# Order of the memory's products in a hybrid layer: values first, and the keys' norm and transposes inside the first attention step

## The chip, the cores and the metric

One NeuronCore of a Trainium2 chip runs the whole program; the seven others are idle. The metric is the time of one execution on the device in microseconds (us). The kernel before takes 1273.12 us, the median of three runs.

## The reference

One layer of a streaming encoder on x (512 rows of 1024 features) with a memory of 256 rows. In float32:

```python
x = x + 0.5 * swiglu(rmsnorm(x, ffn1_norm), ...)          # feed-forward 1
h = rmsnorm(x, mix_norm)
aq, ak, av, bq, bk, bv, cq = split(h @ w_in)
o_a = diff_attention(rope(norm(aq)), rope(norm(ak)), av, lam)  # A, block-causal
o_b = chunk_band_attention(norm(bq), norm(bk), bv, b_rel_bias) # B, band of chunks
mk, mv = split(rmsnorm(mem, mem_norm) @ w_mem_kv, 2)      # memory: keys, values
o_c = memory_attention(norm(cq), norm(mk), mv)            # C: 4 heads of 128
gates = sigmoid(h @ w_gate + b_gate)
x = x + (sum of gates * (branches @ w_branch)) @ w_out
x = x + 0.5 * swiglu(rmsnorm(x, ffn2_norm), ...)          # feed-forward 2
return rmsnorm(x, final_norm)
```

`norm` is an RMS norm of each head with a gain. `lam` is one number, made from two dot products of learned vectors.

## The kernel before

**Products.** Every float32 operand of a product is held as two parts, a high part (`whi`, `mwh`, `fh`, `hh`, ...) that ACT casts (L77) and a low part that DVE gets by subtracting (L78). A product is three matmuls (`mm3`, L110 to L112): high by high, and the two mixed ones. Weights come by DMA from SyncE's queue into a ring of six raw buffers (`wraw`), are split, and used.

**Stages.** Feed-forward 1 is first. In its last part each row block t of x (128 rows, four of them) is finished by DVE (L271, `x_sb`), and `row_mix` at once makes that block's norm for the attentions: square on ACT (L137), `ms` on DVE (L156), the power -1/2 on POOL (`rs`, L121), the scaled row `xn` on DVE (L141, two halves), two groups of four transposes on PE into banks "t" (L149), and the split of these into `hh` (ACT) and `hl` (DVE). The memory's rows were normed earlier and lie transposed in `mh`, `ml`.

Then come three products with a helper, `rows_product`, which takes weights in four chunks: the memory's keys (`mk_ps`, two row tiles in the two banks "s", 48 matmuls of 512 columns), the attention queries against the memory (`cq_ps`, four row tiles in banks "p", "g", "g", "o", 96 matmuls), and the memory's values (`mv_ps`, again the two banks "s", 48 matmuls). Keys and cq are normed by head (`norm4`): a square on ACT (L576), a sum on DVE (L578, `hss`), `msh` on DVE (L127), a power on POOL (L121, `rsh`), the scaling on DVE, which reads the bank (L580), and the gain on DVE (L586). `heads_T` (L593) transposes a normed tile on PE and splits it, for the keys into `mkh`, `mkl`. L618 to L624 make `lam`. ACT copies the values out of their banks (L629).

**The order of the work.** On PE the attentions stand in an order written out by hand: strings like PLAN_C0 name what PE does in one step of a unit. `p4` is four steps of the unit's projection (three matmuls of 384 columns each), `f2` two steps of the gates and branches (three matmuls of 512 columns each), and `c.qt`, `c.sc`, `c.sc2`, `c.pt`, `c.pv` are the stages of one row block of the memory attention: transposes of cq, scores of two heads, scores of the other two, transposes of the probabilities, product with the values. PLAN_C0 is the string of the first unit's step, step 0. Everything else, the rows above among it, is ordered by the Tile scheduler, engine by engine; inside `tc.high_priority(offset=AHEAD)` an instruction is ranked 600 places earlier. Each engine runs its list in that order, and what an instruction must wait for is set by the tiles that it reads, and by the banks and buffers that it takes over (banks: "s" 2, "g" 2, "p" 1, "o" 1, "t" 2).

Of the kernel before, what the change touches and what calls it, by code (L numbers as in the profile page):

```python
# [11 lines left out]
F32 = mybir.dt.float32  # L12
# [6 lines left out]
P = 128  # L19
# [7 lines left out]
NMT = NM // P  # L27
EPS = 1e-6
NEG = -1e30
AHEAD = 600  # L30


PLAN_C0 = "p2 c.qt p2 c.sc p2 f4 c.sc2 p3 f2 c.qt f2 c.pt f4 c.pv"
PLAN_C = "c.sc f1 p2 u.ot c.ot p2 u.pt c.sc2 p2 u.qt p3 c.qt f1 u.sc f1 c.pt f1 u.pv f1 c.pv"
PLAN_A = "c.sc p2 c.ot c.sc2 p3 u.pt p2 u.qt u.ot p2 c.pt f2 u.sc f1 u.pv c.pv f3"
PLAN_B = "p5 u.pt p2 u.qt u.ot p2 f1 u.sc f1 u.pv f4"
# [11 lines left out]
def layer_kernel(ctx: ExitStack, tc: tile.TileContext, a: dict, out: bass.AP):  # L48
    nc = tc.nc

    base = ctx.enter_context(tc.tile_pool(name="base", bufs=1))
# [8 lines left out]
    def bank(tag):  # L60
        return pp.tile([P, 512], F32, tag=tag, name="ps_" + tag, bufs=BANKS[tag])
# [13 lines left out]
    def split(raw, hi, lo, engine=None):  # L75

        nc.scalar.copy(out=hi, in_=raw)  # L77
        (engine or nc.vector).tensor_tensor(out=lo, in0=raw, in1=f32(hi), op=ALU.subtract)  # L78
# [22 lines left out]
    def weight(src, n, pool=None, tags=("whi", "wlo"), bufs=4, raw=None, engine=None):  # L101
        if raw is None:
            raw = load(src, n)
        hi, lo = ((pool or base).tile([P, 1024], F32R, tag=t, name=t, bufs=bufs)[:, :n] for t in tags)
        split(raw, hi, lo, engine)
        return hi, lo

    def mm3(ps, st, mv, first, last):

        nc.tensor.matmul(ps, lhsT=st[0], rhs=mv[0], start=first, stop=False)  # L110
        nc.tensor.matmul(ps, lhsT=st[0], rhs=mv[1], start=False, stop=False)  # L111
        return nc.tensor.matmul(ps, lhsT=st[1], rhs=mv[0], start=False, stop=last)  # L112
# [201 lines left out]
    class Job:  # L314


        def __init__(self, prep, run, blocks=1):
            self.prep, self.run, self.blocks = prep, run, blocks
# [233 lines left out]
    h2, mT = mix_in["h"], mix_in["mT"]  # L552
# [3 lines left out]
    mem_pool = memp.__enter__()  # L556

    def heads(ap, n):
        return ap.rearrange("p (h d) -> p h d", h=n)


    def rows_product(acc, actT, w, c0, **where):

        for c in range(4):
            wc = weight(w[c * 256:(c + 1) * 256, c0:c0 + 512].rearrange("(k p) n -> p k n", p=P), 1024, **where)
            for t, ps in enumerate(acc):
                for j in range(2):
                    k, o = 2 * c + j, slice(j * 512, j * 512 + 512)
                    mm3(ps, tuple(m[:, k, t * P:(t + 1) * P] for m in actT), (wc[0][:, o], wc[1][:, o]),
                        k == 0, k == ND - 1)  # L570
        return acc

    def head_norm(src, dst, sq):

        nh, hd = src.shape[1], src.shape[2]
        nc.scalar.activation(out=sq, in_=src, func=AF.Square)  # L576
        ss = tiny("hss", nh)
        nc.vector.tensor_reduce(out=ss, in_=sq, axis=AX.X, op=ALU.add)  # L578
        rs = rsqrt_mean(ss, nh, 1.0 / hd, "h")
        nc.vector.tensor_tensor(out=dst, in0=src, in1=rs.unsqueeze(2).broadcast_to([P, nh, hd]), op=ALU.mult)  # L580

    def norm4(ps, yn, sq, gain):

        head_norm(heads(ps, 4), heads(yn, 4), heads(sq, 4))
        v = heads(yn, 4)
        nc.vector.tensor_tensor(out=v, in0=v, in1=gain.unsqueeze(1).broadcast_to([P, 4, 128]), op=ALU.mult)  # L586
        return yn

    def heads_T(yn, dst, cols):

        ps = bank("t")
        for h in range(4):
            nc.tensor.transpose(ps[:, h * P:(h + 1) * P], yn[:, h * P:(h + 1) * P], ident)  # L593
        split(heads(ps, 4), dst[0][:, :, cols], dst[1][:, :, cols])

    mem_w = dict(pool=mem_pool, tags=("mwh", "mwl"), bufs=2)
    gck, gcq = (mem_pool.tile([P, P], F32, name="gc" + n) for n in "kq")
    for g, n in ((gck, "k"), (gcq, "q")):
        nc.sync.dma_start(out=g, in_=a[f"c_{n}_norm"].partition_broadcast(P))
    mkT = [base.tile([P, 4, NM], F32R, tag="w4", name=n, bufs=2) for n in ("mkh", "mkl")]  # L600
    mk_ps = rows_product([bank("s") for _ in range(NMT)], mT, a["w_mem_kv"], 0, **mem_w)
    for t in range(NMT):
        yn = mem_pool.tile([P, 512], F32, tag="mk", name="mk", bufs=3)
        sq = mem_pool.tile([P, 512], F32, tag="mk", name="mksq", bufs=3)
        heads_T(norm4(mk_ps[t], yn, sq, gck), mkT, slice(t * P, (t + 1) * P))
    cq_ps = rows_product([bank(t) for t in ("p", "g", "g", "o")], h2, a["w_in"], 3072)
    y_sb = base.tile([P, ND, S], F32, tag="xy", name="y_sb")

# [1 line left out]
    for t in range(NT):  # L610
        sq = mem_pool.tile([P, 512], F32, tag="mk", name="cqsq", bufs=3)
# [11 lines left out]

    nc.vector.tensor_scalar(out=nlam, in0=le[:, 1:2], scalar1=-LAMBDA_INIT, scalar2=le[:, 0:1],  # L624
                            op0=ALU.add, op1=ALU.subtract)
    mv_ps = rows_product([bank("s") for _ in range(NMT)], mT, a["w_mem_kv"], 512, **mem_w)
    mv = base.tile([P, NMT, 512], F32, tag="kx", name="mv", bufs=2)
    for t in range(NMT):
        nc.scalar.copy(out=mv[:, t, :], in_=mv_ps[t])  # L629
    memp.__exit__(None, None, None)  # L630
    mix_in["mTp"].__exit__(None, None, None)
    norm_pool[0] = (base, "raw", 6)
# [9 lines left out]
    def bcast(name, src, n):  # L642
        g = mp.tile([P, n], F32, name=name)
        nc.sync.dma_start(out=g, in_=src.partition_broadcast(P))
        return g

    gsub = bcast("gsub", a["a_sub_norm"], 128)
    nc.vector.tensor_scalar(out=gsub, in0=gsub, scalar1=1.0 - LAMBDA_INIT, scalar2=None, op0=ALU.mult)
    gb = mp.tile([P, 2, 64], F32, name="gb")
# [23 lines left out]

    def p_tile(name):
        return mp.tile([P, 512], F32, tag="p", name=name, bufs=4)

    def pT_tile(name):
        return mp.tile([P, 512], F32, tag="pT", name=name, bufs=2)
# [10 lines left out]
    def new_oT(name):  # L689

        return (mo.tile([P, 4, S], F32R, tag="oh", name=name + "h", bufs=2),
                mo.tile([P, 4, S], F32R, tag="ol", name=name + "l", bufs=2))
# [12 lines left out]
    class MemStep:  # L705
# [16 lines left out]
        def scores(self, hp):  # L722
            s_ps = bank("g")
            sv = heads(s_ps, 2)
            for j in range(2):
                h = 2 * hp + j
                mm3(sv[:, j, :], tuple(v[:, h, :] for v in self.cq), (mkT[0][:, h, :], mkT[1][:, h, :]), True, True)
            nm = tiny("nm", 2)
            nc.vector.tensor_reduce(out=nm, in_=sv, axis=AX.X, op=ALU.max, negate=True)
            nc.vector.tensor_scalar(out=nm, in0=nm, scalar1=C_SCALE, scalar2=None, op0=ALU.mult)  # L730
            pt = p_tile("p")
            for j in range(2):
                h = 2 * hp + j
                nc.scalar.activation(out=heads(pt, 2)[:, j, :], in_=sv[:, j, :], func=AF.Exp, scale=C_SCALE,
                                     bias=nm[:, j:j + 1], accum_out=self.sum[:, h:h + 1])
            self.pts.append(pt)
# [214 lines left out]
    def advance(gen, n):  # L951
        for _ in range(n):
            next(gen, None)
# [8 lines left out]
    def due(kind, stage):  # L962

        most = 1 if stage == "qt" and kind == "c" else NT
        steps = todo[kind, stage][:most]
        del todo[kind, stage][:most]
        for st in steps:
            with tc.high_priority(offset=AHEAD):
                getattr(st, stage)()
            if stage in nxt[kind]:  # L970
                todo[kind, nxt[kind][stage]].append(st)

    def born(kind, step):
        todo[kind, "qt"].append(step)

    def run(step, plan):

        work = {"p": step.proj() if step else fill, "f": fill}
        for item in plan.split():
            if "." in item:  # L980
                due(*item.split("."))
            else:
                advance(work[item[0]], int(item[1:]))
        if step:
            born("u", step)
# [19 lines left out]
    with tc.manual_schedule(engines={mybir.EngineType.PE}):  # L1005
# [3 lines left out]
        for u in range(8):  # L1009
            un = Unit(u)  # L1010
            for i in range(NT):
                if u in (0, 4) and i == 2:
                    oTs.append(new_oT("o" + "ab"[u // 4]))
                run(UnitStep(un, i), (PLAN_C0 if i == 0 else PLAN_C) if u == 0 else PLAN_A if u < 4 else PLAN_B)
        for _ in range(3):
# [112 lines left out]
```

## Time and profile before

| what | value |
|---|---|
| median of 3 runs | 1273.12 us (1272.8 to 1274.1) |
| the profiled execution | 1273.05 us |
| its span | 1271.3 us |
| mean granted clock of TensorE | 0.987 |
| PE busy | 1232.4 us, 97% |
| DVE, ACT, POOL busy | 842.8, 596.8, 107.1 us |
| chain that ended last | PE 90%, DVE 4%, DMA 2% |

The span runs from the first to the last instruction on the core; 1.75 us of the execution lie outside it. A timeline has one line per instruction, or per run of like ones: start, duration, engine, line, operation, tile written and tiles read, and in brackets the idle time of the engine before it and what released it. Durations of one engine overlap a little at the ends, so what one of several costs is the distance from start to start. The granted clock is a share of full speed: 1.00 is 2.4 GHz, 0.50 is 1.2 GHz.

### The profile page before, as it was taken

What the parts mean: (1) busy time and instruction counts of PE and PEld (TensorE: products, weight loads), DVE (VectorE), ACT (ScalarE), POOL (GpSimd) and SP (SyncE); (2) the same over time, 40 slices, a digit from 0 to 9 for tenths busy, and PEclk for the clock granted to TensorE, in tenths of its full rate; (3) what the DMA queues carried; (4) which work ended last, traced back from release to release, by engine and by line L of the source; (5) the groups of instructions that cost most, each with busy time, mean ns of one, the idle gap of its engine ahead of it and who ended that gap; (6) DMA issues with size and microseconds to landing.
All of it is one profiled execution on the core that took longest, in us unless ns stands there. A gap on an engine that the chain in (4) does not pass through costs nothing.

```text
span 1271.3 us, 19657 instructions
## 1 busy us (share of the span) xinstructions
PE 1232.4 (97%) x7808; PEld 1116.9 (88%) x7808; DVE 842.8 (66%) x1377; ACT 596.8 (47%) x1115; POOL 107.1 (8%) x108
## 2 busy tenths in 40 slices
PE   7799999999998999999999999999979999999997
PEld 7789989989986799999999999888878998998996
DVE  7977667667564756766765565453697766766753
ACT  7535425435443446554555454443463452543543
POOL 1100000000000301111221121020000000000002
PEclk8899999999999899999999999999989999999999
DMA  5533324322334403321222320254133242342311
GB/s 215 174 108 116 115 71 128 113 91 101 116 118 130 109 28 108 88 67 58 88 87 70 89 83 31 75 159 160 34 127 122 76 133 91 101 129 73 130 35 67
DMA packets 53084, 127.57 MB, mean 100 GB/s; under 512 B 10112, under 2 KB 10624, under 8 KB 52992
## 3 DMA queue, kind: packets, MB, share of 16 engines
q1 hardware_dynamic: 52416, 125.27, 30.9%
q8 instruction: 61, 1.00, 0.3%
q10 hardware_dynamic: 576, 1.05, 0.2%
q14 instruction: 31, 0.25, 0.1%
HBM read 122.11 MB, written 4.19 MB: 99 GB/s over the span
## 4 chain that ended last, share of the span: by engine, by line
PE 90%; DVE 4%; DMA 2%; ACT 1%; POOL 1%; issue 1%; SPq 0%; POOLq 0%; ACTq 0%; DVEq 0%
PE ps_s L354 19%; PE ps_g L110 9%; PE ps_g L112 9%; PE ps_g L111 9%; PE ps_o L354 5%; PE ps_p L110 4%; PE ps_p L354 4%; PE ps_p L111 4%; PE ps_p L112 4%; PE ps_g L354 4%; PE ps_s L110 2%; PE ps_s L112 2%; PE ps_s L111 2%; PE ps_o L881 2%; PE ps_s L849 2%; PE ps_t L697 1%
## 5 line engine op out<-in xcount | busy, mean ns | idle before, releaser
L77 ACT CAST whi<-wraw 128x1024 fp32r<-128x1024 f32 (+1 forms) x120 | 119.0, 993 | 141.3 <-PE ps_s L354 68.6
L78 DVE TENSOR_TENSOR wlo<-wraw,whi 128x1024 fp32r<-128x1024 f32 (+1 forms) x120 | 137.9, 1151 | 65.6 <-ACT whi L77 64.6
L354 PE MATMUL ps_s<-mhi,whi 128*128 128x256 f32 x496 | 138.3, 279 | 2.3 <-ACT snap L397 2.0
L354 PE MATMUL ps_s<-mlo,whi 128*128 128x256 f32 x496 | 137.7, 278 | 0.0
L354 PE MATMUL ps_s<-mhi,wlo 128*128 128x256 f32 x496 | 136.8, 278 | 0.0
L77 ACT CAST whi<-quarter 128x1024 fp32r<-128x1024 f32 x54 | 56.7, 1051 | 91.8 <-PE ps_s L354 22.7
L354 PEld LDWEIGHTS ps_s<-mhi,whi 128*128 128x128 f32 x496 | 93.8, 189 | 4.1 <-ACT snap L397 2.8
L110 PE MATMUL ps_p<-whi,hh 128*128 128x384 f32 (+1 forms) x264 | 94.8, 359 | 0.0
L354 PEld LDWEIGHTS ps_s<-mlo,whi 128*128 128x128 f32 x496 | 93.7, 189 | 1.0 <-DVE mlo L78 0.2
L354 PEld LDWEIGHTS ps_s<-mhi,wlo 128*128 128x128 f32 x496 | 93.2, 189 | 0.0
L112 PE MATMUL ps_p<-whi,hl 128*128 128x384 f32 (+1 forms) x264 | 89.2, 338 | 0.0
L111 PE MATMUL ps_p<-wlo,hh 128*128 128x384 f32 (+1 forms) x264 | 89.2, 338 | 0.0
L78 DVE TENSOR_TENSOR wlo<-quarter,whi 128x1024 fp32r<-128x1024 f32 x54 | 65.9, 1221 | 24.5 <-ACT whi L77 24.5
L110 PE MATMUL ps_g<-hh,fh 128*128 128x512 f32 x192 | 78.4, 408 | 0.0
L112 PE MATMUL ps_g<-hh,fl 128*128 128x512 f32 x192 | 75.8, 395 | 0.0
L111 PE MATMUL ps_g<-hl,fh 128*128 128x512 f32 x192 | 75.7, 394 | 0.0
L834 DVE CAST kx<-ps_t 128x256 fp32r<-128x256 f32 x32 | 13.6, 425 | 83.7 <-PE ps_t L832 83.7
L121 POOL TENSOR_TENSOR rsh<-msh,mhalf 128x4 f32<-128x4 f32 x38 | 45.2, 1191 | 276.9 <-DVE msh L127 225.2
L78 DVE TENSOR_TENSOR fl<-wraw,fh 128x768 fp32r<-128x768 f32 x48 | 50.0, 1042 | 26.1 <-ACT fh L77 26.1
L77 ACT CAST fhi<-quarter 128x1024 fp32r<-128x1024 f32 x34 | 35.5, 1049 | 59.1 <-PE ps_s L354 16.4
L354 PE MATMUL ps_s<-mhi,fhi 128*128 128x256 f32 x208 | 59.2, 285 | 2.5 <-ACT fhi L77 2.5
L354 PE MATMUL ps_s<-mlo,fhi 128*128 128x256 f32 x208 | 58.9, 283 | 0.0
(376 smaller groups left out, 3662.8 us busy)
## 6 DMA issues: line engine op xcount, KB each, us to landing
wraw<-in_ffn_w SPq DMA_DIRECT2D x88, 512.0 KB, 4.0
wraw<-in_ffn_wd SPq DMA_DIRECT2D x44, 512.0 KB, 3.9
wraw<-in_w_u SPq DMA_DIRECT2D x32, 384.0 KB, 3.3
wraw<-in_w_gb SPq DMA_DIRECT2D x32, 384.0 KB, 3.0
wraw<-in_w_gf SPq DMA_DIRECT2D x16, 384.0 KB, 3.1
wraw<-in_w_mem_kv SPq DMA_DIRECT2D x8, 512.0 KB, 4.1
wraw<-in_w_out SPq DMA_DIRECT2D x8, 512.0 KB, 4.5
x_sb<-in_x SPq DMA_DIRECT2D x4, 512.0 KB, 7.0
```

The costliest lines, as they stand in the source:

```text
L77: nc.scalar.copy(out=hi, in_=raw)
L78: (engine or nc.vector).tensor_tensor(out=lo, in0=raw, in1=f32(hi), op=ALU.subtract)
L110: nc.tensor.matmul(ps, lhsT=st[0], rhs=mv[0], start=first, stop=False)
L111: nc.tensor.matmul(ps, lhsT=st[0], rhs=mv[1], start=False, stop=False)
L112: return nc.tensor.matmul(ps, lhsT=st[1], rhs=mv[0], start=False, stop=last)
L121: nc.gpsimd.tensor_tensor(out=rs, in0=ms, in1=mhalf[:, :n], op=ALU.pow)
L354: nc.tensor.matmul(ps[:, c], lhsT=x, rhs=y, start=first and j + k + n == 0, stop=k == 3 and n == 2, skip_group_check=True)
L697: nc.tensor.transpose(ps[:, j * P:(j + 1) * P], pt[:, j * P:(j + 1) * P], ident)
L834: nc.vector.tensor_copy(out=un.kx[:, :, qs], in_=heads(p2[:, 0:256], 2))
L849: nc.tensor.matmul(out_, lhsT=q, rhs=k, start=j == 0, stop=j == 1)
L881: nc.tensor.matmul(o[:, vs], lhsT=pT[:, j * P:(j + 1) * P], rhs=un.v[:, j, vs], start=j == 0, stop=j == i)
```

## The change

The values' product moves ahead of the keys'; ACT's copies of the values free the two banks "s", and the keys follow into them. The keys' gain `gck` moves to the pool of the attentions, behind the other weights on SyncE's queue. The keys' norm moves behind the setup of the attentions, into tiles "p", under high priority; their transposes become an item "mk" of PLAN_C0, which is written anew.

```diff
-PLAN_C0 = "p2 c.qt p2 c.sc p2 f4 c.sc2 p3 f2 c.qt f2 c.pt f4 c.pv"
+PLAN_C0 = "p4 c.qt p5 mk f6 c.sc f2 c.sc2 f2 c.qt f1 c.pt f1 c.pv"
...
-    gck, gcq = (mem_pool.tile([P, P], F32, name="gc" + n) for n in "kq")
-    for g, n in ((gck, "k"), (gcq, "q")):
-        nc.sync.dma_start(out=g, in_=a[f"c_{n}_norm"].partition_broadcast(P))
+    gcq = mem_pool.tile([P, P], F32, name="gcq")
+    nc.sync.dma_start(out=gcq, in_=a["c_q_norm"].partition_broadcast(P))
     mkT = [base.tile([P, 4, NM], F32R, tag="w4", name=n, bufs=2) for n in ("mkh", "mkl")]
+
+    mv_ps = rows_product([bank("s") for _ in range(NMT)], mT, a["w_mem_kv"], 512, **mem_w)
+    mv = base.tile([P, NMT, 512], F32, tag="kx", name="mv", bufs=2)
+    for t in range(NMT):
+        nc.scalar.copy(out=mv[:, t, :], in_=mv_ps[t])
     mk_ps = rows_product([bank("s") for _ in range(NMT)], mT, a["w_mem_kv"], 0, **mem_w)
-    for t in range(NMT):
-        yn = mem_pool.tile([P, 512], F32, tag="mk", name="mk", bufs=3)
-        sq = mem_pool.tile([P, 512], F32, tag="mk", name="mksq", bufs=3)
-        heads_T(norm4(mk_ps[t], yn, sq, gck), mkT, slice(t * P, (t + 1) * P))
...
-    mv_ps = rows_product([bank("s") for _ in range(NMT)], mT, a["w_mem_kv"], 512, **mem_w)
-    mv = base.tile([P, NMT, 512], F32, tag="kx", name="mv", bufs=2)
-    for t in range(NMT):
-        nc.scalar.copy(out=mv[:, t, :], in_=mv_ps[t])
...
+    gck = bcast("gck", a["c_k_norm"], 128)
     gsub = bcast("gsub", a["a_sub_norm"], 128)
...
+    with tc.high_priority(offset=AHEAD):
+        mk = [norm4(mk_ps[t], p_tile("mk"), p_tile("mksq"), gck) for t in range(NMT)]
+
+    def mk_transposed():
+        with tc.high_priority(offset=AHEAD):
+            for t in range(NMT):
+                heads_T(mk[t], mkT, slice(t * P, (t + 1) * P))
...
         for item in plan.split():
-            if "." in item:
+            if item == "mk":
+                mk_transposed()
+            elif "." in item:
```

What this does to the engines' lists, at three places. First PE at the end of feed-forward 1 (numbers in names tell tiles apart; `ps_g_3940` is ffn1's last bank, `xn_4027`, `xn_4069` and `xn_4111` are rows 1, 2 and 3 of x). Before:

```order
L112 MATMUL ps_g_3940<-whi_3955,gl_2956 128x512
L110 MATMUL ps_p_4250<-whi_4256,hh_3874 128x512
L111 MATMUL ps_p_4250<-wlo_4257,hh_3874 128x512
L149 MATMUL ps_t_4029<-ident_80,xn_4027 128x128 x4
L112 MATMUL ps_p_4250<-whi_4256,hl_3875 128x512
L110 MATMUL ps_p_4250<-whi_4256,hh_3874 128x512
L111 MATMUL ps_p_4250<-wlo_4257,hh_3874 128x512
L112 MATMUL ps_p_4250<-whi_4256,hl_3875 128x512
L149 MATMUL ps_t_4037<-ident_80,xn_4027 128x128 x4
```

And with the change:

```order
L112 MATMUL ps_g_3940<-whi_3955,gl_2956 128x512
L149 MATMUL ps_t_4029<-ident_80,xn_4027 128x128 x4
L149 MATMUL ps_t_4037<-ident_80,xn_4027 128x128 x4
L149 MATMUL ps_t_4071<-ident_80,xn_4069 128x128 x4
L149 MATMUL ps_t_4079<-ident_80,xn_4069 128x128 x4
L149 MATMUL ps_t_4113<-ident_80,xn_4111 128x128 x4
L149 MATMUL ps_t_4121<-ident_80,xn_4111 128x128 x4
L110 MATMUL ps_s_4138<-mwh_4142,mh_3879 128x512
L110 MATMUL ps_s_4139<-mwh_4142,mh_3879 128x512
L111 MATMUL ps_s_4138<-mwl_4143,mh_3879 128x512
```

The six groups of transposes stood between products of cq (`ps_p_4250`); now they follow ffn1's last matmul in one row, and the values' product (`ps_s_4138`, `ps_s_4139`) comes behind them. On ACT the same place with the change reads (`hh_3874` are the transposed rows of x, `mwh_4142` the first weight chunk of the values):

```order
L77 CAST hh_3874<-ps_t_4071 128x4x128
L77 CAST hh_3874<-ps_t_4079 128x4x128
L77 CAST hh_3874<-ps_t_4113 128x4x128
L77 CAST hh_3874<-ps_t_4121 128x4x128
L77 CAST mwh_4142<-wraw_4140 128x1024
```

The first cast of a weight of the values stands behind the last cast of x's rows. Third, DVE with the change, up to the first key tile's gain (`y_sb_4413` are the rows of cq, `mk_4497` is the first key tile, `y2_4593`, `yb_4594` and `squ_4584` belong to unit 0):

```order
L620 TENSOR_REDUCE le_4457<-lam_4454 128x2
L586 TENSOR_TENSOR y_sb_4413<-y_sb_4413,gcq_4134 128x512
L580 TENSOR_TENSOR y_sb_4413<-ps_o_4292,rsh_4450 128x512
L814 TENSOR_TENSOR yb_4594<-ps_p_4550,sg_4483 128x4x32 x2
L816 TENSOR_TENSOR y2_4593<-ps_p_4550,cg_4482 128x256
L580 TENSOR_TENSOR mk_4497<-ps_s_4215,rsh_4504 128x512
L578 TENSOR_REDUCE hss_4511<-mksq_4509 128x4
L800 TENSOR_REDUCE hss_4587<-squ_4584 128x4
L624 TENSOR_SCALAR le_4457<-le_4457 128x1
L586 TENSOR_TENSOR y_sb_4413<-y_sb_4413,gcq_4134 128x512
L817 TENSOR_TENSOR y2_4593<-y2_4593,yb_4594 128x256
L586 TENSOR_TENSOR mk_4497<-mk_4497,gck_4469 128x512
```

Before, the first key tile's gain stood ahead of all norms of cq; now it stands behind all of them, behind `lam` and behind unit 0's first operations. On PE its transposes come here (`ps_p_4550` is unit 0's projection, `ps_g_4618` the first gate):

```order
L110 MATMUL ps_p_4550<-whi_4543,hh_3874 128x384
L111 MATMUL ps_p_4550<-wlo_4544,hh_3874 128x384
L112 MATMUL ps_p_4550<-whi_4543,hl_3875 128x384
L593 MATMUL ps_t_4604<-ident_80,mk_4497 128x128 x4
L593 MATMUL ps_t_4611<-ident_80,mk_4508 128x128 x4
L110 MATMUL ps_g_4618<-hh_3874,fh_4621 128x512
```

They stand between the projection's last matmul and the first gate; before, they stood among the products of the values.

## Rows read from the trace of the kernel before

**Rows 1.** Part 1 of the page: busy time, share of the span, instructions.
```profile
PE 1232.4 (97%) x7808; PEld 1116.9 (88%) x7808; DVE 842.8 (66%) x1377; ACT 596.8 (47%) x1115; POOL 107.1 (8%) x108
```

**Rows 2.** Timeline of PE at the end of ffn1 and through cq's product.
```profile
372.10 0.39 PE L112 MATMUL ps_g<-whi,gl 128*128 128x512 f32 x1
372.33 0.39 PE L110 MATMUL ps_p<-whi,hh 128*128 128x512 f32 x1
...
372.79 0.60 PE L149 MATMUL ps_t<-ident,xn 128*128 128x128 f32 x4
373.15 0.48 PE L112 MATMUL ps_p<-whi,hl 128*128 128x512 f32 x1
...
386.75 0.60 PE L149 MATMUL ps_t<-ident,xn 128*128 128x128 f32 x4
```

**Rows 3.** Timeline of PE, the first matmul of c.sc in step 1.
```profile
448.30 0.37 PE L110 MATMUL ps_g<-mkh,cqh 128*128 128x256 f32 x1
```

**Rows 4.** Timeline of PE, the first products of the values.
```profile
413.98 0.76 PE L110 MATMUL ps_s<-mwh,mh 128*128 128x512 f32 x1 [5.57 <-DVE mk L580]
414.54 0.63 PE L111 MATMUL ps_s<-mwl,mh 128*128 128x512 f32 x1
...
418.80 0.63 PE L112 MATMUL ps_s<-mwh,ml 128*128 128x512 f32 x1
```

**Rows 5.** Windows: length, then PE, PEld, DVE, ACT, POOL busy; granted clock, DMA share, GB/s.
```profile
413.00:419.00 6.00, 5.03 (x12) 3.99 (x13) 4.70 (x10) 1.19 (x2) 1.84 (x3) 0.50 0.34 120
```

**Rows 6.** Timeline of DVE, ACT and POOL: x's last row, the first memory weights.
```profile
374.52 0.68 DVE L271 SCALAR_TENSOR_TENSOR x_sb<-ps_g,x_sb 128x512 f32<-128x512 f32 x1
...
375.30 0.60 ACT L137 ACTIVATE ps_g<-x_sb 128x512 f32<-128x512 f32 x1
...
376.66 0.55 POOL L121 TENSOR_TENSOR rs<-ms,mhalf 128x1 f32<-128x1 f32 x1 [5.91 <-DVE ms L156]
...
377.25 1.41 DVE L141 SCALAR_TENSOR_TENSOR xn<-x_sb,rs,gain 128x512 f32<-128x512 f32 x2 [0.73 <-POOL rs L121]
...
387.38 0.59 ACT L77 CAST hh<-ps_t 128x512 fp32r<-128x512 f32 x1 [1.01 <-PE ps_t L149]
387.86 2.00 ACT L77 CAST mwh<-wraw 128x1024 fp32r<-128x1024 f32 x2
...
388.94 2.36 DVE L78 TENSOR_TENSOR mwl<-wraw,mwh 128x1024 fp32r<-128x1024 f32 x2 [0.26 <-ACT mwh L77]
```

**Rows 7.** Timeline of DVE, back to back in cq's norms.
```profile
428.05 0.28 DVE L620 TENSOR_REDUCE le<-lam 128x2 f32<-128x128 f32 x1
428.24 0.68 DVE L586 TENSOR_TENSOR y_sb<-y_sb,gcq 128x512 f32<-128x512 f32 x1
428.84 0.68 DVE L580 TENSOR_TENSOR y_sb<-ps_o,rsh 128x512 f32<-128x512 f32 x1
```

**Rows 8.** Windows at two other falls of the clock, at the start and in ffn2.
```profile
9.00:13.00 4.00, 1.25 (x8) 0.84 (x8) 3.01 (x5) 4.00 (x10) 0.55 (x1) 1.00 1.02 417
13.00:14.00 1.00, 0.00 (x0) 0.00 (x0) 1.00 (x3) 1.00 (x4) 0.00 (x0) 0.68 1.02 410
...
930.00:932.00 2.00, 1.41 (x6) 1.42 (x7) 2.00 (x3) 1.97 (x3) 0.00 (x0) 0.50 0.00 0
...
934.00:935.00 1.00, 1.00 (x6) 1.00 (x6) 1.00 (x3) 1.00 (x2) 0.00 (x0) 0.52 0.43 66
```

**Rows 9.** Window in the values' product, with cq's norms on DVE.
```profile
420.00:430.00 10.00, 10.00 (x52) 8.50 (x51) 9.37 (x19) 5.53 (x8) 3.11 (x3) 1.00 0.35 99
```

**Rows 10.** Timeline of DVE and POOL: powers of the keys' norm, and what ran beside.
```profile
411.28 0.95 DVE L78 TENSOR_TENSOR wlo<-wraw,whi 128x768 fp32r<-128x768 f32 x1
411.45 1.65 POOL L121 TENSOR_TENSOR rsh<-msh,mhalf 128x4 f32<-128x4 f32 x1 [34.24 <-DVE msh L127]
...
415.18 1.01 POOL L121 TENSOR_TENSOR rsh<-msh,mhalf 128x4 f32<-128x4 f32 x1 [2.08 <-DVE msh L127]
416.23 0.69 DVE L580 TENSOR_TENSOR mk<-ps_s,rsh 128x512 f32<-128x512 f32 x1 [1.13 <-POOL rsh L121]
```

## The prediction

> **What bounds the kernel now.** I read the page first: PE is busy for 97% of the span [rows 1], so time can only come from PE's idle stretches or from stretches at the low clock, and every new wait of PE is paid in full. Then I went to the stretch that the change touches, from the end of ffn1 (last matmul at 372.10 [rows 2]) to the second memory score of the attentions (c.sc of step 1, 448.30 [rows 3]). Before the first of these and behind the second the engines' orders are the same before and after, so the difference of this stretch is the difference of the kernel. It takes 448.30 - 372.33 = 75.97 us.
>
> In the timeline of PE the reader is to see one large hole there: the first product of the values waits 5.57 us for DVE's L580, because the keys' norm still reads the bank "s" that it needs [rows 4]. Behind it the granted clock is 0.50, so 1.2 GHz instead of 2.4 [rows 5], and twelve matmuls stand 0.427 us apart (414.54 to 418.80 in ten steps [rows 4]) where the pitch at full clock is 0.23 (372.10 to 372.33 [rows 2]). The smaller waits of this stretch I leave as they are in my sum.
>
> At the end of ffn1 there is no hole, though x's norm is still at work: the products of cq run between the transposes of rows 1 to 3 of x, the first at 372.79, the last at 386.75 [rows 2]. There are six groups, 0.36 us each (372.79 to 373.15).
>
> **What the change removes.** The values come first and ACT copies them out of bank "s" in two copies of the known L629 kind; 17 matmuls of cq (4 us) stand between the values' last product and the keys' first, so nothing waits for the bank. Gone: 5.57 us of waiting and 12 x (0.427 - 0.23) = 2.3 us of slow clock. Together **-7.9 us**. The broadcast of gck, moved behind the weights on SP's queue, is wanted only by the keys' gain, ten microseconds after the products end: nothing. The number of matmuls, transposes, casts and norm operations is the same: nothing.
>
> **What it adds at the end of ffn1 (place A).** PE's new order has the six groups of transposes directly behind ffn1's last matmul, and behind them the values. The products of cq, which covered them, now come after the values. So PE meets the whole chain of x's last row bare. Its steps, by the trace of before: from x_sb (374.52) by the square (375.30), POOL's power (376.66) and xn (377.25 + 1.41) it takes 4.14 us [rows 6]. It now starts when ffn1's last matmul ends, 372.10 + 0.39 = 372.5 [rows 2], so xn is done at 376.65. DVE then has two pieces hl of row 2 at 0.60 each (the pitch of 512-wide operations on DVE, 428.24 to 428.84 [rows 7]) before both banks "t" are free, to 377.9; the last transposes follow, and two casts hh at 0.48 (387.38 to 387.86 [rows 6]) on ACT, to 379.2. The first weight of the values is cast behind these on ACT, 1.0 us (2.00 for two [rows 6]), to 380.2; its low part takes DVE 1.18 (2.36 for two [rows 6]), and PE is under way from 381.6. Of these 9.27 us since 372.33, work is 6 x 0.36 + 2 x 0.23 plus their changes of shape, 2.8: **+6.5 us** idle.
>
> Does the clock fall? PE is busy for a third of this stretch. At the start of the program PE was busy for 1.25 of 4 us and the clock fell right behind it, to a mean of 0.68 in the next microsecond [rows 8]. So I say it falls. After another idle stretch the low clock lasted from a start at 930.59 (1.41 us busy to 932) to about 935, 4.4 us [rows 8]; behind the 5.57 us it lasted from 413.98 to 419 or a little past [rows 5]. In 4.4 us at 0.427 instead of 0.23 per matmul 2.0 us are lost, and 0.3 in transposes that run at half clock: **+2.3 us**, between 0 and 3.0 (6 us low).
>
> **What it adds in unit 0's step (place B).** From 381.6 on, 46 matmuls of the values and 144 of cq and the keys at 0.2325 bring PE to 425.8 without a wait. The projection's first matmul waits for bank "p", which cq's first L580 must have read, and later for a weight's low part: **+0.6 us**. Its 24 matmuls (384 wide, 0.17 each, an estimate from 512 columns in 0.23) and one group of transposes of cq end at 431.1. Then the plan's item "mk" wants the keys' gained rows. In before, DVE worked off the norms of cq while PE had the values to do: in 420 to 430 it was busy for 9.4 of 10 us [rows 9]. Now both norms, lambda and the unit's own chain stand in DVE's queue at once. From the first L127 of cq at 425.9 to the gain L586 of the first key tile I count 26 instructions: 14 of 512 elements at 0.60 [rows 7] are 8.4 us, one weight difference 768 wide 0.9 [rows 10], and eleven small ones at 0.2 (428.05 to 428.24 [rows 7]) 2.2. So DVE is at 425.9 + 11.5 = 437.4, and PE waits from 431.1 to 437.5: **+6.4 us**. The second key tile: its L127, POOL's power 1.0, then L580, the first tile's mkl and L586 at 0.60, so PE goes on at 440.7 where 0.7 of the time was transposes: **+2.5 us**. After 6.4 us idle the clock is low, as behind the 5.57 us of before; from 440.7 to about 445 that costs **+1.8 us** (2.6 if it lasts as long as behind 413.98).
>
> What that power costs is the one price with two values: 1.65 us where DVE was busy beside it (411.45), 1.01 where DVE was idle (415.18 to 416.23 [rows 10]). Here DVE has only a short L127 and then waits for this power, so I take 1.01. [...]
>
> **Sum:** -7.9 + 6.5 + 2.3 + 0.6 + 6.4 + 2.5 + 1.8 = **+12.2 us**. The profiled execution took 1273.05 us (span 1271.3 and 1.75 around it); its median of three runs is 1273.12, the same within 0.01%. So 1273.05 + 12.2 = 1285.2; I forecast **1285 us**. A measurement can tell about 0.2%, 2.5 us.
>
> **Rivals.**
> - The clock holds at A. For it: A has no single hole as long as the 5.57 us of before, its idle time is cut up by the transposes. Against it: the rows of the program's start, where eight operations in 4 us did not hold it [rows 8]. Then 1285.2 - 2.3 = **1282.9**.
> - DVE keeps up at B. The point that decides is whether the gain L586 of the first key tile ends by 431.1. It would if most of the 26 instructions were done under the last 58 products of cq, which follow the keys' last one. For it: the keys' own sums are ready before cq's. Against it: the new order puts cq's norms ahead of the keys' on DVE, and those wait for cq's last products. Then 6.4 + 2.5 + 1.8 fall away: **1274.5**, not slower than before by what can be told; with the clock holding at A too, 1272.2.
> - Both low clocks last 6 us and the power takes 1.65: +0.7, +0.8, +0.65, so **1287.4**.
>
> **How the numbers follow.** Forecast 0.55; clock holds at A 0.29; DVE keeps up 0.05; the long case 0.08; 0.03 for something not seen. The range reaches from 1279.5 (the clock holds at A and DVE's small instructions take half of what I gave them, with a short low clock behind B) to 1288. Faster by over 0.2%: 0.02, since A alone pays back most of what goes. Within 0.2%: 0.04, DVE keeping up. Slower by over 0.2%: 0.94.
>
> **What would show it.** Right: the timeline of PE has no wait for L580 at the values; it has instead a row of waits at the six L149 groups and at the first values product, 6 to 7 us together, released by xn, hh and mwh; a granted clock of 0.50 behind them; then a wait of some 6 us at the first transposes of the keys, released by DVE's L586, and one of 2 to 3 us at the second; c.sc of step 1 near 460 instead of 448.3. Wrong: values products between the L149 groups, or the key transposes with less than 2 us of waiting, or a new wait behind 460 that neither kernel has in this sum.

## The result, and the profile after

The changed kernel takes 1283.41 us (median of 4 runs, 1283.11 to 1284.92) against 1273.61 for the kernel before beside it (1272.8 to 1275.68): the ratio is 1.0077, 95% interval 1.0059 to 1.0094, so 9.8 us slower. The forecast was 1285.

The stretch of the prediction, from ffn1's last matmul to c.sc of step 1, went from 76.2 us (372.10 to 448.30) to 86.9 (372.11 to 459.05), 10.7 more. Behind it the two traces need the same: 823.0 and 822.75 us. So the difference of the kernels lies in this stretch. The largest waits of PE in it, in the changed kernel (released tile, line, by what: us in total, times, longest):

```profile
PE ps_t L593 <- DVE mk L586: 8.4, 2, 6.3
PE ps_t L149 <- DVE hl L78: 2.7, 3, 1.3
PE ps_s L110 <- ACT mwh L77: 1.6, 1, 1.6
PE ps_g L110 <- ACT y_sb L923: 0.8, 1, 0.8
PE ps_s L111 <- DVE mwl L78: 0.5, 1, 0.5
```

The 5.57 us for L580 [rows 4] are gone. In their place stand two groups: the key transposes, which wait for the gain L586, and the end of ffn1, where x's transposes wait for hl and the values for their first weight.

Place A is the timeline of PE behind ffn1's last matmul, where rows 2 of before have products of cq:

```profile
372.11 0.40 PE L112 MATMUL ps_g<-whi,gl 128*128 128x512 f32 x1
372.35 1.03 PE L149 MATMUL ps_t<-ident,xn 128*128 128x128 f32 x8
374.35 0.66 PE L149 MATMUL ps_t<-ident,xn 128*128 128x128 f32 x4 [0.96 <-DVE hl L78]
375.44 0.66 PE L149 MATMUL ps_t<-ident,xn 128*128 128x128 f32 x4 [0.44 <-DVE hl L78]
377.37 1.25 PE L149 MATMUL ps_t<-ident,xn 128*128 128x128 f32 x8 [1.27 <-DVE hl L78]
380.24 0.73 PE L110 MATMUL ps_s<-mwh,mh 128*128 128x512 f32 x2 [1.62 <-ACT mwh L77]
381.50 0.50 PE L111 MATMUL ps_s<-mwl,mh 128*128 128x512 f32 x1 [0.53 <-DVE mwl L78]
```

From 372.35 to 381.50 are 9.15 us with 2.7 us of work (six groups at 0.36, two products at 0.23). The brackets add up to 4.8 only, since a lone group's line lasts 0.66 us where the next would start after 0.36. The windows (columns as in rows 5; the last but two is the granted clock) show a clock that held through the idle time and fell when products ran again:

```profile
372.00:382.00 10.00, 5.18 (x31) 3.44 (x30) 7.92 (x13) 5.92 (x10) 0.55 (x1) 1.00 0.16 59
382.00:383.00 1.00, 1.00 (x4) 0.80 (x4) 0.58 (x1) 0.00 (x0) 0.00 (x0) 0.69 0.23 35
383.00:385.00 2.00, 2.00 (x6) 1.55 (x5) 0.00 (x0) 0.00 (x0) 0.00 (x0) 0.50 0.81 284
...
386.00:387.00 1.00, 1.00 (x6) 0.82 (x5) 0.47 (x1) 0.50 (x1) 0.00 (x0) 1.00 0.39 148
```

Place B, PE from the end of cq's product to c.sc of step 1:

```profile
427.10 0.34 PE L110 MATMUL ps_p<-whi,hh 128*128 128x384 f32 x1
...
431.54 0.33 PE L112 MATMUL ps_p<-whi,hl 128*128 128x384 f32 x1
438.16 1.11 PE L593 MATMUL ps_t<-ident,mk 128*128 128x128 f32 x4 [6.29 <-DVE mk L586]
441.41 1.09 PE L593 MATMUL ps_t<-ident,mk 128*128 128x128 f32 x4 [2.13 <-DVE mk L586]
442.14 0.78 PE L110 MATMUL ps_g<-hh,fh 128*128 128x512 f32 x1
...
446.99 0.51 PE L112 MATMUL ps_g<-hh,fl 128*128 128x512 f32 x1
...
459.05 0.37 PE L110 MATMUL ps_g<-mkh,cqh 128*128 128x256 f32 x1
```

And what DVE does meanwhile, from the first L127 of cq on; it is back to back from cq's first scaling to the first key tile's gain:

```profile
424.53 0.17 DVE L127 TENSOR_SCALAR msh<-hss 128x4 f32<-128x4 f32 x1
...
425.83 0.69 DVE L580 TENSOR_TENSOR y_sb<-ps_p,rsh 128x512 f32<-128x512 f32 x1
...
433.52 0.68 DVE L580 TENSOR_TENSOR y_sb<-ps_o,rsh 128x512 f32<-128x512 f32 x1
...
434.85 0.68 DVE L580 TENSOR_TENSOR mk<-ps_s,rsh 128x512 f32<-128x512 f32 x1
...
437.42 0.68 DVE L586 TENSOR_TENSOR mk<-mk,gck 128x512 f32<-128x512 f32 x1
438.02 0.23 DVE L127 TENSOR_SCALAR msh<-hss 128x4 f32<-128x4 f32 x2
439.37 0.69 DVE L580 TENSOR_TENSOR mk<-ps_s,rsh 128x512 f32<-128x512 f32 x1 [1.12 <-POOL rsh L121]
```

The key tile's gain comes after everything of cq, and PE, which was done at 431.7, starts the transposes right behind it.

One question the prediction left open: why does the Tile scheduler put cq's products behind the memory's? The queue of SyncE tells. The first loads of cq's weights, in the changed kernel and then in before:

```profile
387.79 7.54 SPq L98 DMA_DIRECT2D wraw<-in_w_in  x4
```

```profile
339.61 5.72 SPq L98 DMA_DIRECT2D wraw<-in_w_in  x2
```

With the change all four weight chunks of cq are issued at 387.8 or later. The values' four chunks and the keys' four stand ahead of them, and the ring has six raw buffers; in before only the keys' four did, and two chunks of cq were loaded while ffn1 still ran. Run e1 tests this.

### The profile page after: what moved, and what is told of

It reads as the page before. It is cut to its first block, busy times and chain, and to the rows that moved or that the text cites. A ratio compares the mean times of both kernels' runs of the same rounds, so it can differ in the third digit from the quotient of the medians.

```text
span 1281.8 us, 19655 instructions
## 1 busy us (share of the span) xinstructions
PE 1235.2 (96%) x7808; PEld 1119.4 (87%) x7808; DVE 844.0 (66%) x1377; ACT 597.8 (47%) x1115; POOL 103.3 (8%) x108
## 4 chain that ended last, share of the span: by engine, by line
PE 65%; DVE 4%; ACT 1%; issue 0%; POOL 0%; POOLq 0%; ACTq 0%; DVEq 0%
PE ps_s L354 9%; PE ps_g L110 8%; PE ps_g L112 7%; PE ps_g L111 7%; PE ps_p L110 4%; PE ps_p L112 4%; PE ps_p L111 4%; PE ps_o L354 2%; PE ps_p L354 2%; PE ps_g L354 2%; PE ps_s L111 2%; PE ps_o L886 2%; PE ps_s L112 2%; PE ps_s L110 2%; PE ps_s L854 2%; PE ps_t L702 1%
## 5 line engine op out<-in xcount | busy, mean ns | idle before, releaser
L839 DVE CAST kx<-ps_t 128x256 fp32r<-128x256 f32 x32 | 13.6, 425 | 83.7 <-PE ps_t L837 83.7
L77 ACT CAST fh<-wraw 128x768 fp32r<-128x768 f32 x48 | 39.9, 833 | 43.5 <-PE ps_g L111 29.6
```

Of the source, the lines that this page charges most:

```text
L839: nc.vector.tensor_copy(out=un.kx[:, :, qs], in_=heads(p2[:, 0:256], 2))
```

## The experiments

Stretch means the time from ffn1's last matmul to c.sc of step 1 in the profiled execution; it leaves out that the runs reach ffn1's end up to 1.6 us apart. Each ratio is worked out from all runs against runs of before that were taken beside them (their median is 1273.28 us for e1 to e4 and 1273.79 for e5 and e6), so it is not always the quotient of two medians of the table.

| kernel | median, us | ratio to before, 95% interval | stretch, us |
|---|---|---|---|
| before | 1273.61 | | 76.2 |
| the change | 1283.41 | 1.0077 (1.0059 to 1.0094) | 86.9 |
| e1, cq's first weights early | 1277.9 | 1.0035 (1.0021 to 1.005) | 80.5 |
| e2, values first, nothing else | 1276.25 | 1.0014 (1.0003 to 1.0026) | 79.2 |
| e3, mk behind f6 | 1279.91 | 1.0057 (1.0042 to 1.0072) | 84.0 |
| e4, cq between, mk behind f6 | 1272.32 | 0.9997 (0.9988 to 1.0006) | 75.7 |
| e5, e4 with early small loads | 1268.06 | 0.9953 (0.994 to 0.9965) | 72.1 |
| e6, e5 with mk at once | 1273.82 | 1.0 (0.9991 to 1.0009) | 78.4 |
| e7, the change, three gains less | 1284.33 (one run) | | 84.9 |

**e1: place A undone alone.** The order of the products in the code is the change's; only two loads move.

```diff
-    def rows_product(acc, actT, w, c0, **where):
+    def rows_product(acc, actT, w, c0, raws=(), **where):
...
-            wc = weight(w[c * 256:(c + 1) * 256, c0:c0 + 512].rearrange("(k p) n -> p k n", p=P), 1024, **where)
+            wc = weight(chunk_src(w, c0, c), 1024, raw=raws[c] if c < len(raws) else None, **where)
...
+    early = [load(chunk_src(a["w_in"], 3072, c), 1024) for c in range(2)]
     mk_ps = rows_product([bank("s") for _ in range(NMT)], mT, a["w_mem_kv"], 0, **mem_w)
-    cq_ps = rows_product([bank(t) for t in ("p", "g", "g", "o")], h2, a["w_in"], 3072)
+    cq_ps = rows_product([bank(t) for t in ("p", "g", "g", "o")], h2, a["w_in"], 3072, raws=early)
```

> The changed kernel with one thing different: the first two weight chunks of cq are loaded ahead of the keys' four, so they get two of the six raw buffers while ffn1 still runs. Theory (the loss has two places, and place A exists because the eight memory chunks stand ahead of cq's in the ring): 48 products of cq now stand between the six transpose groups, the 9.2 us from ffn1's last matmul to the values shrink to work, A's 6.5 us of idle time and its 1.6 us of low clock go, place B stays with waits of about 6.3 and 2.1 us; some 1.0 us come back because transposes between products cost more than in a row. 1283.4 - 7.1 = 1276 us (1275 to 1278). Rival (what A loses is only moved: DVE, POOL and the small loads set when B ends): B's first wait grows to 13 us or more, 1281 to 1284.

The stretch fell by 6.4 us. With two chunks loaded the scheduler by itself put 48 products of cq ahead of the values, 36 of them ahead of the last group of transposes; from 372 to 422 every window has PE busy throughout at a clock of 1.00, and the largest waits are these:

```profile
PE ps_t L596 <- DVE mk L589: 9.6, 2, 7.0
PE ps_g L110 <- ACT y_sb L927: 0.8, 1, 0.8
```

(L589 and L596 are L586 and L593 of the change.) So place A exists because of the ring, as expected. The rival is right in a small part: B's waits grew from 8.4 to 9.6. From the end of cq's product to the end of the first key tile's gain there are 11.9 us (420.23 to 432.09) instead of 11.0 (427.10 to 438.10); DVE's queue there now has scalings of the small tiles in it and a wait of 0.96 for lambda's exponential. 1277.9 lies at the upper end of what was expected.

**e2: place B undone alone.** The diff is against the kernel before; the lines removed stood behind `lam`.

```diff
+    mv_ps = rows_product([bank("s") for _ in range(NMT)], mT, a["w_mem_kv"], 512, **mem_w)
+    mv = base.tile([P, NMT, 512], F32, tag="kx", name="mv", bufs=2)
+    for t in range(NMT):
+        nc.scalar.copy(out=mv[:, t, :], in_=mv_ps[t])
     mk_ps = rows_product([bank("s") for _ in range(NMT)], mT, a["w_mem_kv"], 0, **mem_w)
```

> The kernel before with the values' product and copies moved ahead of the keys' and nothing else: the old PLAN_C0, the keys' norm and transposes right behind their product. Theory: place A as in the changed kernel (9.2 us from ffn1's last matmul to the values, low clock behind it), no place B, since DVE norms the keys before cq's rows and their transposes stand among cq's last products; the 5.57 us wait for L580 is gone. 1283.4 less B's 6.45 + 3.3 + 2.1 = 11.8 is 1271.6; with a wait of half a microsecond at bank p 1271 to 1274. Rival (B is not DVE's order but DVE's load: the same 26 instructions must be done before the scores anyway): a wait of 5 us or more appears at the projection's bank or at c.sc, 1277 to 1282.

B's transposes run among cq's last products without a wait, and the stretch is 7.7 us shorter than the change's. But 1276.25 is over the 1271 to 1274 expected. Two things are in the trace: the scores wait for DVE after all, with a low clock from 436 to 439.5 behind it, and at A the clock fell earlier than in the change's profile, before the values began (at 382.0), and came back later. PE's two waits and two windows:

```profile
434.84 0.38 PE L111 MATMUL ps_g<-mkl,cqh 128*128 128x256 f32 x1 [1.46 <-DVE mkl L78]
435.71 0.40 PE L112 MATMUL ps_g<-mkh,cql 128*128 128x256 f32 x1 [0.49 <-DVE cql L78]
```

```profile
379.00:381.00 2.00, 1.39 (x7) 0.99 (x5) 0.69 (x1) 1.16 (x3) 0.00 (x0) 0.50 0.15 38
387.00:388.00 1.00, 1.00 (x4) 0.81 (x3) 0.00 (x0) 0.06 (x1) 0.00 (x0) 0.50 0.82 305
```

The rival is right in part: the scores wait 2.0 us for DVE where it said 5 or more. The ten runs also spread in step with the granted clock: four lie between 1272.69 and 1274.19 us at a mean of 0.987, near what was expected, and six between 1275.99 and 1277.94 at 0.981 to 0.985; the profile is of one of the six (1276.9). The gain of moving the values ahead alone is eaten by place A.

**e3: the six gate steps ahead of mk.**

```diff
-PLAN_C0 = "p4 c.qt p5 mk f6 c.sc f2 c.sc2 f2 c.qt f1 c.pt f1 c.pv"
+PLAN_C0 = "p4 c.qt p5 f6 mk f2 c.sc f2 c.sc2 c.qt f1 c.pt f1 c.pv"
```

> The changed kernel with the plan item mk behind the six gate steps and two more gate steps behind it (p4 c.qt p5 f6 mk f2 c.sc f2 c.sc2 c.qt f1 c.pt f1 c.pv); the same work. Theory: 18 gate products, 4.2 us at full clock, run in B's hole; the first key transposes wait 2.2 us instead of 6.3, the second 2.1 to 2.6, the low clock costs 0 to 2.6. 1276 to 1278.5 us. Rival (the scores or their split become the wait: mkl behind the transposes): what the first wait loses comes back at c.sc, 1281 to 1284.

The first wait is 2.17 us as expected, the second 3.17, a microsecond more than the change's 2.13. Some 0.4 of that is only that the first transposes ran at full clock here (0.66 us instead of 1.11), so that the wait began earlier; from start to start the second group came 3.83 us behind the first (440.69 to 444.52) instead of the change's 3.25. The reason for these 0.6 stands in the timelines of DVE and POOL: a weight's low part slipped in ahead of the second tile's power, and the two powers took 2.57 us where the change's took 1.98.

```profile
440.63 0.94 DVE L78 TENSOR_TENSOR fl<-wraw,fh 128x768 fp32r<-128x768 f32 x1
```

```profile
440.86 2.57 POOL L121 TENSOR_TENSOR rsh<-msh,mhalf 128x4 f32<-128x4 f32 x2 [5.25 <-DVE msh L127]
```

This is the case that the Trainium skill describes in "SBUF — State Buffer", section "SBUF: two separate sides": a DVE operation with two SBUF inputs that has begun shuts a GpSimd operation that reads SBUF out until it ends. The trace agrees: the power began at 440.86 behind the subtraction, which ended at 441.57, and the price is the difference between the two values that the prediction gave for a power, about 0.6 us.

**e4: cq's product between the values' and the keys'.** The change with one line moved and the plan of e3.

```diff
+    cq_ps = rows_product([bank(t) for t in ("p", "g", "g", "o")], h2, a["w_in"], 3072)
     mk_ps = rows_product([bank("s") for _ in range(NMT)], mT, a["w_mem_kv"], 0, **mem_w)
-    cq_ps = rows_product([bank(t) for t in ("p", "g", "g", "o")], h2, a["w_in"], 3072)
```

> The changed kernel with cq's product written between the values' and the keys', and the plan of the run before (mk behind f6). Theory: A is covered by cq's products as in the kernel before; the keys come last, after DVE has done cq's norms beside the values, so the first key tile's gain is done some 4.1 us behind the keys' last product, and the 4.2 us of gate products cover it; no wait over 1 us between 372 and c.sc of step 1, full clock throughout. 1273.1 - 8 = 1265.5 us (1264.5 to 1268). Rival (the keys' norm behind the last product costs what it cost before, 5.6 us and a low clock): 1271 to 1273.

A is covered and DVE is done with cq's norms at 413, but the time is only that of before: a miss by 7 us. It lies in the rival's range, but not for the rival's reason: the two groups of key transposes follow each other within 0.79 us (436.84 to 437.63). PE waits at the first gate, and DVE names the cause, a small load that comes late and holds the weight behind it:

```profile
430.92 0.80 PE L112 MATMUL ps_g<-hh,fl 128*128 128x512 f32 x1 [3.21 <-DVE fl L78]
```

```profile
429.80 0.20 DVE L651 TENSOR_SCALAR ga<-ga 128x64 f32<-128x64 f32 x1 [2.51 <-DMA ga<-in_a_q_norm]
429.91 1.82 DVE L78 TENSOR_TENSOR fl<-wraw,fh 128x768 fp32r<-128x768 f32 x2
431.65 0.68 DVE L580 TENSOR_TENSOR mk<-ps_s,rsh 128x512 f32<-128x512 f32 x1
```

The keys' scaling stands behind the same load. The small loads begin with gck at 422.08, and this is what stands before it in SyncE's queue, and on DVE:

```profile
421.70 0.33 SPq L98 DMA_DIRECT2D wraw<-in_w_u  x1
422.08 0.43 SPq L640 DMA_DIRECT2D gck<-in_c_k_norm  x1
```

```profile
420.45 1.23 DVE L78 TENSOR_TENSOR mwl<-wraw,mwh 128x1024 fp32r<-128x1024 f32 x1 [2.61 <-ACT mwh L77]
```

gck comes right after the memory's last low weight (mwl) is done at 421.68. Two things would give that time: a weight load (`w_u`) stands ahead of gck in the queue and waited for this low weight, and gck's tile lies in a pool that is opened behind the memory's weights. Which of the two held it was not separated.

**e5: e4 with the small tiles in a pool of their own, opened ahead of the memory's weights.**

```diff
     memp.__exit__(None, None, None)
+    small = tc.tile_pool(name="small", bufs=1, reuse_waits="tile")
+    sp_ = small.__enter__()
...
+    gck = bcast("gck", a["c_k_norm"], 128)
+    gsub = bcast("gsub", a["a_sub_norm"], 128)
...
     memp = tc.tile_pool(name="memw", bufs=1, reuse_waits="tile")
```

> The run e4 with one thing more: the small loads of the attentions (gck, gsub, ga, gb, cg, sg, hb) and what scales them stand in a pool of their own ahead of the memory's weights, so that they are loaded while cq's product runs. In e4 DVE stood 2.5 us at ga's load with the first gate's low weight behind it, and PE waited 3.2 us for that weight, with a low clock behind. Theory (that wait, and nothing of the keys' norm, is what kept e4 from its gain): the wait at the first gate falls to 1 us or less, the key transposes wait under 1 us, no low clock; the stretch from ffn1's last matmul to c.sc of step 1 goes from 75.7 to 71 us, the time to 1268 us (1266.5 to 1270). Rival (the keys' norm itself, last in line, takes the wait over at the first key transposes): 1271 to 1273.

The small loads now come earlier in the code and in the queue (gck at 382.45) as well as in a pool of their own, so e5 shows that their lateness cost e4 its gain, and not which of the two made them late. 1268.06 us: the expected time, and faster than both kernels. The largest waits left in the stretch:

```profile
PE ps_g L110 <- ACT fh L77: 1.2, 1, 1.2
PE ps_g L110 <- ACT p L741: 0.7, 1, 0.7
PE ps_g L112 <- DVE fl L78: 0.6, 1, 0.6
PE ps_g L111 <- DVE mkl L78: 0.5, 1, 0.5
```

The key transposes hardly wait: their two groups take 1.11 us (433.10 to 434.21) where 0.72 is work. A short low clock remains, against what was expected (0.78 in the window 425 to 430). Of the 5.3 us that the profiled span gains over before's the stretch gives 4.1; behind it the trace is 2.2 us shorter than before's (820.8 against 823.0), and ahead of it 1.0 longer. These two were not followed.

**e6: e5 with the plan of the change.**

```diff
-PLAN_C0 = "p4 c.qt p5 f6 mk f2 c.sc f2 c.sc2 c.qt f1 c.pt f1 c.pv"
+PLAN_C0 = "p4 c.qt p5 mk f6 c.sc f2 c.sc2 f2 c.qt f1 c.pt f1 c.pv"
```

> The run e5 with the plan of the change (mk right behind the projection, ahead of the six gate steps). Theory: the keys' last product is directly followed by their transposes, so the whole norm of the keys is bare: about 6 us at the first transposes, 1 us at the second, a low clock of some 2 us behind: 1273 us (1271 to 1275), 4 to 6 us over e5. Rival (the position of mk in the plan matters little once DVE is free of cq's norms): within 1.5 us of e5.

```profile
431.14 1.09 PE L628 MATMUL ps_t<-ident,mk 128*128 128x128 f32 x4 [5.92 <-DVE msh L127]
434.31 1.08 PE L628 MATMUL ps_t<-ident,mk 128*128 128x128 f32 x4 [2.09 <-DVE mk L621]
```

(L628 is L593 of the change.) 1273.82, 5.8 us over e5, as expected. So the keys' norm costs some 6 us bare even when cq's norms are done. That is not the length of its own steps: DVE is still back to back, with unit 0's operations and with low parts of the gates' weights, such as these two ahead of the first key tile's scaling (L615, which is L580 of the change):

```profile
426.72 0.95 DVE L78 TENSOR_TENSOR fl<-wraw,fh 128x768 fp32r<-128x768 f32 x1
...
427.93 0.95 DVE L78 TENSOR_TENSOR fl<-wraw,fh 128x768 fp32r<-128x768 f32 x1
428.79 0.68 DVE L615 TENSOR_TENSOR mk<-ps_s,rsh 128x512 f32<-128x512 f32 x1
```

From the first key tile's sum (424.72) to the end of its gain (430.99) are 6.3 us, of which its own operations and POOL's power are 3.2. With this queue the six gate steps must stand before mk, not behind it; a DVE queue with the keys' norm ahead of those operations was not run.

**e7: three operations less in DVE's queue.**

```diff
-        norm4(cq_ps[t], c_rows[:, t, :], sq, gcq)
+        norm4(cq_ps[t], c_rows[:, t, :], sq, gcq if t == 0 else None)
```

> The changed kernel without the gain of cq's rows 1 to 3 (those three rows of queries are left without their gain): three DVE operations of 0.60 us less in the queue ahead of the first key tile's gain, all else as it was. Theory (DVE's queue sets B): the first wait at the key transposes goes from 6.29 to 4.5 us, the second stays at 2.1 to 2.6. Rival (POOL's powers or a load set it): the wait stays over 6.0.

```profile
438.37 1.11 PE L595 MATMUL ps_t<-ident,mk 128*128 128x128 f32 x4 [4.84 <-DVE mk L588]
441.62 1.09 PE L595 MATMUL ps_t<-ident,mk 128*128 128x128 f32 x4 [2.13 <-DVE mk L588]
```

The first wait fell by 1.45 us, the second stayed. Of the 1.8 us taken out, 0.27 came back as a wait of DVE itself, for lambda's exponential. So DVE's queue sets the first wait of B. The stretch is 2.0 us shorter; the one time that was taken is no measure of that.

## Why the prediction was right

Step by step, with the measured terms of the profile after:

| step | predicted, us | measured, us |
|---|---|---|
| wait and low clock at the values | -7.9 | -8.4, both gone (5.74 from 408.01 to 413.98 less one product, 2.6 from there to 419.74) |
| A, idle | +6.5 | +6.5 (9.15 less 2.7 of work) |
| A, low clock | +2.3 | +1.6 (eight matmuls at 0.43, 382.7 to 385.9) |
| bank p and a late weight | +0.6 | 0 (the projection starts at 427.10 behind cq's last product) |
| B, first key tile | +6.4 | +6.45 (431.71 to 438.16) |
| B, second key tile | +2.5 | +3.3 (to 442.14, less 0.7 of work) |
| B, low clock | +1.8 | +2.3 (11 matmuls in 4.85 us at 442.14 to 446.99) |
| sum | +12.2 | +11.8 |
| the stretch | | +10.7 |

**The two places** are where the prediction had them, and for its reasons: e1 takes away A and 6.4 us, e2 takes away B and 7.7, e5 both and 14.8. They do not simply add up: A's 8.1 us are gone in e1, but B's waits grew by 1.2 there, and in e2 the scores began to wait. The two large terms, read from DVE's row of instructions and from x's last row, came out within 0.1 us. For A that is the chain itself: PE was under way from 381.50 where 381.6 was expected, though at the transposes hl released it last and not xn. **For B it is in part luck.** The first L127 of cq was forecast at 425.9, with the end of cq's product; it stood at 424.53, 2.6 us ahead of that end (427.10). From it to the end of the gain (438.10) there were 13.6 us instead of the 11.5 that were counted, since 30 instructions stood there and not 26, among them 16 of 512 elements and not 14. The early start and the longer queue nearly cancelled; the 0.6 that was left met a PE that came 0.6 later too (431.71 instead of 431.1).

**What failed** is the smaller half. The late banks and weights cost nothing: cq's first scaling stood at 425.83, before the projection asked for the bank at 427.10. The second key tile cost 0.8 more: its transposes began 3.25 us behind the first tile's (438.16 to 441.41), near the 3.2 of the sum, and POOL's power in it took the 1.0 that was taken (two in 1.98 us from 438.33); but the sum ended there and left out the 0.73 that they then took themselves, at half clock. The clock of A was forecast to fall in the idle stretch; in this profile it fell at about 382.4, 0.9 us after the products ran on at 381.50. And the sum of terms is 1.1 us over what the stretch lost, because the prediction left out how evenly the same work runs. In before each of the six groups of x's transposes stands alone among products, and the product behind such a group is 0.31 us from the next instead of 0.23 (373.15 to 373.46), 0.5 us in all; in a row they do not cost this. Before's first scores, six products, take 1.47 us up to 432.63, with a wait of 0.22 in them; the change's take 0.71 (448.71 to 449.42). The words "The number of matmuls, transposes, casts and norm operations is the same: nothing." are right on the number, but should not have set this term to nothing. What was removed was also half a microsecond dearer than the 7.9 of the sum, which took the wait from its bracket (5.57): from start to start the wait and its low clock, between these two lines of before's PE, come to 8.4 (11.73 less thirteen products at 0.23 and a group at 0.36):

```profile
408.01 0.39 PE L112 MATMUL ps_s<-mwh,ml 128*128 128x512 f32 x1
...
419.74 0.48 PE L110 MATMUL ps_s<-mwh,mh 128*128 128x512 f32 x1
```

The forecast of 1285 is 1.6 us high, and the errors, of up to about 1 us each, partly cancelled.

**The rivals.** In the change's profile the clock held at A in the sense that it did not fall in the idle time, but its price was paid behind it; in the profiles of e2, e3 and e7 it fell in the idle stretch, as forecast. So the rival is nearer to wrong. DVE did not keep up at B, and by e7 its queue set the first wait. The long case did not come.

## What to carry to other kernels

Before a product is moved ahead of another, look whose loads take the ring's buffers: here eight chunks ahead of cq's in a ring of six left PE without products exactly where a norm's chain had been covered by them. The cost of a norm that moves is not its own length but what stands before it in its engine's list; count the list from the release to the instruction that is waited for (e7, and the 6.3 us of e6 of which 3.2 are the norm's own), and put as much PE work between a product and the use of its norm as that takes (here 4.2 us of gate products were worth 5.8 us, e5 against e6). When a product moves to the end, look at what is loaded behind its weights: in e4 the small loads came late and cost the gain, and in e5 they stood ahead and did not.

## What the runs showed of the hardware that was not expected

The same row of six transposes and first products met a clock that fell at different places: at about 382.4 in the change's profile, 0.9 us after the products ran on, but before the values' products in those of e2, e3 and e7 (0.50 from 378 to 388 in e2), though the instructions were the same and the waits up to the first product of the values agree within 0.02 us. From ffn1's last matmul to the fifteenth product of the values it took 13.8 us in the change, 14.3 in e7, 15.1 in e3 and 15.2 in e2. What A costs therefore differs by more than a microsecond from one profile to another. Why is open; nothing was run for it.

DVE's operations also ran longer beside some of POOL's. In e4 the gain L586 of a key tile took 1.13 us where it takes 0.68 elsewhere, beside POOL's scaling of cg, which began 0.14 us earlier (433.13), and a 768-wide subtraction of the change at 417.18 took 1.42 instead of 0.95 beside POOL's scalings of cg (from 417.05) and sg. PE waited for neither. POOL's small powers did not do this: two of them ran from 431.03 to 433.08 in the change, and the gain L586 that DVE began at 431.53 took its usual 0.68.
